# Output projection of a hybrid layer: both halves at the end in seven Strassen products, with weight sums made during group B

## The chip, the cores and the metric

One core of a Trainium2 chip runs the whole kernel. The metric is the device time of one launch in microseconds (us). The kernel before was run three times: median 1801.79 us, from 1801.08 to 1802.45. A further execution was profiled, and all rows below come from that one.

## The reference, cut to what matters

One layer over 1024 tokens of width 2048, in float32:

```python
xn = rms_norm(h, norm_w)
proj = xn @ w_in                                   # (1024, 2048) @ (2048, 7184)
...                                                # o_a: gated delta rule over 8 heads, gated by z_A
...                                                # o_b: chunked spatial gating over 8 groups, gated by z_B
mix = jnp.concatenate([o_a, o_b], axis=-1) @ w_out # (1024, 2048) @ (2048, 2048)
h = h + mix
return rms_norm(h, final_norm_w)
```

`o_a` (1024 columns) comes from group A, `o_b` (1024 columns) from group B. The change concerns the product with `w_out`, the residual sum and the final norm.

## The kernel before, in words

**Tiling.** Tokens are worked in two halves of 512 (`hf` 0 and 1, `T` = 512), each of four tiles of 128 tokens (`NT` = 4). The contraction of 2048 is cut into 16 steps of 128 (`KT` = 16). Every large product is made in three matmuls per step: each operand is split into a high part (a copy rounded to fp32r, on ACT, line 134) and a low part (source minus high part, on DVE, line 135), and TensorE (PE) adds high by high, high by low and low by high. `split` (lines 132 to 135) does this for 128x512 tiles.

**Stages.** `program` (line 910) runs, for each half, group A (the q, k, v and z columns, pair by pair of heads), group B (24 chunks of `v_b`, then 16 projections for u and z) and `out_phase(hf)`. So the order is A(0), B(0), out(0), A(1), B(1), out(1). Each stage is a generator of chunks: a prep that loads a 256 KB piece of weights and splits it, and an mm that issues its matmuls. `run` (line 211) keeps three preps ahead of the matmuls. A projection is four chunks of 12 matmuls of 128x512 (`project`, line 247).

**Tasks.** All other work (gates, convolutions, the solve and the recurrence of the delta rule, the spatial gating, evacuation of results) is written as generators that `spawn` queues and `tick` (called once or more in each chunk) advances; `yield n` lets n ticks pass. The recurrence of a pair of heads (`task_pair`, line 545) is a chain between PE and DVE: `p` (line 617, PE) reads the state, `vz` (line 620, DVE) follows, `ds` (line 628, PE) uses it, and `state` (line 629, DVE) is updated for the next `p`. The recurrence of the last pair of a half runs while group B's first chunks are multiplied.

**What sets the order.** A build-time scheduler fixes one order of instructions per engine, and each engine works its list in order. SP issues the loads of weights (`w_chunk`, line 182: three raw buffers `wr`, four of `wh` and of `wl`), the loads of x and the stores of `mix`. POOL issues the loads of `fw` and the `swapo` copies. An instruction that waits on SP or DVE holds up all that stands behind it on that engine.

**Buffers.** A tag names a ring of buffers that several users share; the next user of a buffer waits until the last one is done with it. The tags that the change speaks of are `cv` (3 buffers of 256 KB), `bv` (2), `z` (2), `pc` (4), the activation tiles `ah` and `al` (16 each) and `b8` (4 of 1 MB). PSUM has 3 banks for projections, 2 `p1`, 1 `ds` and 2 general ones.

**Output phase.** `out_phase(hf)` (line 839) takes four column blocks (`cb`) by 16 steps `k`; each chunk loads 256 KB of `w_out` (`wro`), splits it (`who`, `wlo`) and issues for each of the four token tiles three matmuls (lines 891 to 893, result `oa`): 768 matmuls of 128x512 per half. In block 0 each step also loads the half's `mix` tile (`mr`, on ACT's queue) and splits it (`mh`, `ml`), once for the half. `task_out` (line 800) evacuates a block: for each token tile it loads the residual (`xres`, SP, tag `z`), adds the PSUM result (DVE, line 806), squares it with a row sum (ACT, line 808), and multiplies by the norm's weight `fw` (POOL, line 810). After the last block come the row scale and the stores (lines 812 to 837). In the second half the last block's last token tile is multiplied at the very end by itself, so that only one tile's finish follows the last matmul.

The functions that the change touches, with the line numbers of the profile:

Of the kernel before, what the change touches and what calls it, by code (L numbers as in the profile page):

```python
# [8 lines left out]
F32 = mybir.dt.float32  # L9
F32R = mybir.dt.float32r  # L10
# [21 lines left out]
def kernel(ctx, tc, x_tok, x_t, w_in, w_v0, w_vb, w_out, conv_w, norm_w, a_log, dt_bias,  # L32
# [84 lines left out]

    mix_d = [dr.tile([2 * H, P, T], F32, name=f"mix_d{i}", bufs=1) for i in range(NHALF)]
# [141 lines left out]
    def first_tiles(hf, xs, env, done):  # L260
# [3 lines left out]
        for q in range(KT // 2):  # L264
# [22 lines left out]
            def mm(ws, q=q):  # L287
                hi, lo, (vh, vl) = ws
                if q == 0:
                    accs.extend(proj_bank(f"first{hf}_{i}") for i in range(3))  # L290
                    accs.extend(ps.tile([P, T], F32, tag="p1", bufs=2, name=f"first{hf}_{i}") for i in (3, 4))
                    accs.append(ps.tile([P, T], F32, tag="ds", bufs=1, name=f"first{hf}_5"))
# [161 lines left out]
    W_EM = 5  # L454

# [308 lines left out]
    def group_b(hf, xs, st):  # L764

        env, sb = {}, {}
        for blk in range(1, 4):
# [32 lines left out]
    def task_out(hf, cb, acc, env, ts):  # L800
        for t in ts:
            h, ss, st = env["h"][t], env["ss"][:, t, :], env["st"][:, t, :]
            xr = wk.tile([P, T], F32, tag="z", bufs=2, name=f"xres{hf}_{cb}_{t}")
            nc.sync.dma_start(xr, x_tok[hf * NT + t, :, cb * T:(cb + 1) * T])
            hs = h[:, cb * T:(cb + 1) * T]
            nc.vector.tensor_tensor(hs, xr, acc[t], op=ALU.add)
            sq = wk.tile([P, T], F32, tag="o", bufs=2, name=f"sqh{hf}_{cb}_{t}")
            nc.scalar.activation(sq, hs, AF.Square, accum_out=ss[:, cb:cb + 1])
            if cb < 3:
                nc.gpsimd.tensor_tensor(hs, hs, env["fw"][cb], op=ALU.mult)  # L810
            if cb == 2:
                nc.vector.tensor_reduce(st[:, 0:1], ss[:, 0:3], axis=AX.X, op=ALU.add)
                nc.vector.tensor_scalar(st[:, 0:1], st[:, 0:1], DM * EPS, None, op0=ALU.add)
            if cb == 3:
                yield 1

                a, m, y, w = (st[:, i:i + 1] for i in range(1, 5))
                nc.vector.tensor_scalar(a, ss[:, 3:4], st[:, 0:1], 1.0 / DM, op0=ALU.add, op1=ALU.mult)
                nc.vector.tensor_scalar(m, ss[:, 3:4], st[:, 0:1], -0.5 / DM, op0=ALU.add, op1=ALU.mult)
                nc.vector.tensor_scalar(y.bitcast(I32), a.bitcast(I32), -0.5, 1597463007.0, op0=ALU.mult, op1=ALU.add)  # L820
                for _ in range(3):
                    nc.vector.scalar_tensor_tensor(w, y, m, y, op0=ALU.mult, op1=ALU.mult)
                    nc.vector.scalar_tensor_tensor(y, w, 1.5, y, op0=ALU.add, op1=ALU.mult)
                r0 = hf * T + t * P
                for q in (0, 2, 1, 3):
                    cs = slice(q * T, (q + 1) * T)
                    if q < 2:
                        nc.scalar.activation(h[:, cs], h[:, cs], AF.Copy, scale=y)
                    elif q == 2:
                        nc.vector.tensor_scalar(h[:, cs], h[:, cs], y, None, op0=ALU.mult)  # L830
                    else:
                        nc.vector.scalar_tensor_tensor(h[:, cs], h[:, cs], y, env["fw"][q], op0=ALU.mult, op1=ALU.mult)
                    if len(ts) == 1:
                        nc.sync.dma_start(out[r0:r0 + P, cs], h[:, cs])
                    elif q % 2:
                        c2 = slice((q - 1) * T, (q + 1) * T)
                        nc.sync.dma_start(out[r0:r0 + P, c2], h[:, c2])

    def out_phase(hf):


        env = {"mx": [], "w": {}}
        end = hf == NHALF - 1
        spare = [("kd", 3), ("gae", 3), ("ut", 2), ("pc", 4), ("cv", 3), ("wq", 2), ("bv", 2), ("rb", 1)]
        spare = [tb for tb in spare for _ in range(tb[1])]

        def keep(k):

            if k >= KT - 4 or k < 2:
                return None  # L850
            return [wk.tile([P, 1, T], F32R, tag=tag, bufs=bufs, name=f"wk{i}_{k}")
                    for i, (tag, bufs) in enumerate(spare[2 * k - 4:2 * k - 2])]

        def prep(cb, k, late):
            if late:
                return env["w"][k]
            w = w_chunk(w_out[cb, k], [P, 1, T], f"o{hf}_{cb}_{k}", keep(k) if end and cb == 3 else None)
            env["w"][k] = w
            if cb == 0:
                mr = wk.tile([P, T], F32, tag="cv", bufs=3, name=f"mr{hf}_{k}")  # L860
                nc.scalar.dma_start(mr, mix_d[hf][k])
                mh = act.tile([P, T], F32R, tag="ah", name=f"mh{hf}_{k}")
                ml = act.tile([P, T], F32R, tag="al", name=f"ml{hf}_{k}")
                split(mh, ml, mr)
                env["mx"].append((mh, ml))
            return w

        def mm(w, cb, k, late, k1):
            hi, lo = w
            if cb == 0 and k == 0:  # L870
                env["h"] = [big.tile([P, DM], F32, tag="b8", name=f"h{hf}_{t}") for t in range(NT)]
                env["ss"] = sm.tile([P, NT, 4], F32, tag="ssh", bufs=1, name=f"ssh{hf}")
                env["st"] = sm.tile([P, NT, 5], F32, tag="sth", bufs=1, name=f"sth{hf}")
                env["fw"] = []
                for c in range(4):
                    f = wk.tile([P, T], F32, tag=("bv", "bv", "kc", "kc")[c], bufs=2, name=f"fw{hf}_{c}")
                    nc.gpsimd.dma_start(f, fn_w[c * T:(c + 1) * T].partition_broadcast(P))
                    env["fw"].append(f)
            if k == 0:
                if cb % 2 == 0:  # L880
                    acc = [proj_bank(f"oa{hf}_{cb}_{t}") for t in range(3)]
                else:
                    acc = [ps.tile([P, T], F32, tag="p1", bufs=2, name=f"oa{hf}_{cb}_{t}") for t in range(2)]
                    acc += [ps.tile([P, T], F32, tag="ds", bufs=1, name=f"oa{hf}_{cb}_2")]
                env["acc"] = acc + [gen_bank(f"oa{hf}_{cb}_3")]
            acc = env["acc"]
            mh, ml = env["mx"][k]
            ts = (NT - 1,) if late else range(NT - 1) if end and cb == 3 and k > 1 else range(NT)
            for t in ts:
# [4 lines left out]
                if t == 1:  # L894
                    tick()
            if k == k1:
                spawn(task_out(hf, cb, acc, env, ts))
            tick()

        def chunk(cb, k, late=False, k1=KT - 1):  # L900
            return (lambda: prep(cb, k, late)), (lambda w: mm(w, cb, k, late, k1))
# [60 lines left out]
```

## Time and profile before

| what | value |
|---|---|
| runs, median (lowest to highest) | 1801.79 us (1801.08 to 1802.45) |
| the profiled execution, its own time | 1797.83 us |
| its span, first to last instruction | 1796.1 us |
| PE busy | 1763.2 us, 98% of the span |
| DVE / ACT / POOL busy | 1152.3 / 731.9 / 265.1 us |
| mean granted clock | 0.997 of full speed |

Busy time is the sum over an engine's instructions; two that overlap in its pipeline count once. The span is shorter than the execution's own time by what lies around the first and last instruction. In the rows, L12 is line 12 of the kernel, `out<-in` are the program's names, and brackets give idle time before an instruction and what ended it. Numbers in buffer names are mostly left out.

### The profile page before, as it was taken

What the parts mean: (1) busy time and instruction counts of PE and PEld (TensorE: products, weight loads), DVE (VectorE), ACT (ScalarE), POOL (GpSimd) and SP (SyncE); (2) the same over time, 40 slices, a digit from 0 to 9 for tenths busy, and PEclk for the clock granted to TensorE, in tenths of its full rate; (3) what the DMA queues carried; (4) which work ended last, traced back from release to release, by engine and by line L of the source; (5) the groups of instructions that cost most, each with busy time, mean ns of one, the idle gap of its engine ahead of it and who ended that gap; (6) DMA issues with size and microseconds to landing.
All of it is one profiled execution on the core that took longest, in us unless ns stands there. A gap on an engine that the chain in (4) does not pass through costs nothing.

```text
span 1796.1 us, 27364 instructions
## 1 busy us (share of the span) xinstructions
PE 1763.2 (98%) x9526; PEld 1488.7 (83%) x9526; DVE 1152.3 (64%) x2797; ACT 731.9 (41%) x1658; POOL 265.1 (15%) x318
## 2 busy tenths in 40 slices
PE   9999999999999999999999899999999999999997
PEld 8778788887998888888898788878889988888886
DVE  7798787988646334433757988979886554344344
ACT  7543544444343223423646445344443432233232
POOL 3210121211201100011302101212012020001110
PEclk9999999999999999999999999999999999999999
DMA  7455344364424434644455453543534243355443
GB/s 235 129 133 143 106 135 135 94 178 115 136 84 120 124 105 136 222 118 126 131 198 141 121 141 103 147 120 106 162 112 135 76 117 116 102 153 169 124 140 138
DMA packets 166458, 239.16 MB, mean 133 GB/s; under 512 B 35472, under 2 KB 68272, under 8 KB 166064
## 3 DMA queue, kind: packets, MB, share of 16 engines
q1 hardware_dynamic: 156704, 215.35, 41.1%
q0 software_dynamic: 4864, 13.67, 3.1%
q10 hardware_dynamic: 4752, 8.40, 1.5%
q8 instruction: 74, 1.21, 0.3%
q14 instruction: 64, 0.52, 0.1%
HBM read 200.61 MB, written 36.73 MB: 132 GB/s over the span
## 4 chain that ended last, share of the span: by engine, by line
PE 79%; DVE 12%; DMA 4%; ACT 2%; issue 2%; SPq 0%; POOL 0%; DVEq 0%; ACTq 0%; POOLq 0%
PE acc L236 14%; PE acc L239 14%; PE acc L237 14%; PE vb L783 8%; PE oa L891 6%; PE oa L893 6%; PE oa L892 6%; DVE wl L135 2%; DVE cv L410 2%; PE ds L628 1%; DMA wr<-w_in 1%; PE p L617 1%; DVE fs L564 1%; DVE fst L562 1%; PE sp L740 1%
## 5 line engine op out<-in xcount | busy, mean ns | idle before, releaser
L236 PE MATMUL acc<-xh,wh 128*128 128x512 f32 x1472 | 591.3, 402 | 1.3 <-ACT wh L134 1.3
L239 PE MATMUL acc<-xh,wl 128*128 128x512 f32 x1472 | 576.4, 392 | 7.0 <-DVE wl L135 6.8
L237 PE MATMUL acc<-xl,wh 128*128 128x512 f32 x1472 | 575.3, 391 | 0.0
L134 ACT CAST wh<-wr 128x512 fp32r<-128x512 f32 x368 | 225.8, 618 | 432.4 <-PE acc L237 319.8
L135 DVE TENSOR_TENSOR wl<-wr,wh 128x512 fp32r<-128x512 f32 x368 | 255.8, 697 | 156.8 <-ACT wh L134 155.4
L239 PEld LDWEIGHTS acc<-xh,wl 128*128 128x128 f32 x1472 | 276.8, 188 | 66.4 <-DVE wl L135 8.5
L236 PEld LDWEIGHTS acc<-xh,wh 128*128 128x128 f32 x1472 | 277.4, 188 | 57.3 <-issue 3.7
L237 PEld LDWEIGHTS acc<-xl,wh 128*128 128x128 f32 x1472 | 277.4, 188 | 51.9 <-issue 0.7
L891 PE MATMUL oa<-who,mh 128*128 128x512 f32 x472 | 183.6, 389 | 0.0
L892 PE MATMUL oa<-wlo,mh 128*128 128x512 f32 x472 | 183.6, 389 | 0.0
L893 PE MATMUL oa<-who,ml 128*128 128x512 f32 x472 | 183.6, 389 | 0.0
L135 DVE TENSOR_TENSOR wlo<-wro,who 128x512 fp32r<-128x512 f32 x118 | 88.4, 751 | 141.5 <-ACT who L134 141.4
L134 ACT CAST who<-wro 128x512 fp32r<-128x512 f32 x118 | 73.0, 620 | 143.8 <-PE oa L893 135.3
L410 DVE SCALAR_TENSOR_TENSOR cv<-pc,cw,cv 128x511 f32<-128x511 f32 (+1 forms) x144 | 108.5, 754 | 8.5 <-ACT cv L407 6.9
L783 PE MATMUL vb<-whvb,xh 128*128 128x256 f32 x384 | 110.5, 288 | 0.0
L783 PE MATMUL vb<-whvb,xl 128*128 128x256 f32 x384 | 108.6, 283 | 0.0
L783 PE MATMUL vb<-wlvb,xh 128*128 128x256 f32 x384 | 108.6, 283 | 0.0
L892 PEld LDWEIGHTS oa<-wlo,mh 128*128 128x128 f32 x472 | 88.6, 188 | 18.6
L893 PEld LDWEIGHTS oa<-who,ml 128*128 128x128 f32 x472 | 88.6, 188 | 18.4
L891 PEld LDWEIGHTS oa<-who,mh 128*128 128x128 f32 x472 | 88.6, 188 | 18.2
L564 DVE TENSOR_TENSOR fs<-fs,fst 32x31 f32<-32x31 f32 (+15 forms) x248 | 89.2, 360 | 4.1
L562 DVE TENSOR_TENSOR fst<-fs 32x31 f32<-32x31 f32 (+15 forms) x248 | 88.9, 359 | 4.2
(239 smaller groups left out, 2369.6 us busy)
## 6 DMA issues: line engine op xcount, KB each, us to landing
wr<-w_in SPq DMA_DIRECT2D x368, 256.0 KB, 3.1
wro<-w_out SPq DMA_DIRECT2D x128, 256.0 KB, 2.7
wrvb<-w_vb SPq DMA_DIRECT2D x48, 256.0 KB, 2.7
xr<-x_t SPq DMA_DIRECT2D x32, 256.0 KB, 3.7
mr<-mix_d ACTq DMA_DIRECT2D x32, 256.0 KB, 3.2
xres<-x_tok SPq DMA_DIRECT2D x32, 256.0 KB, 3.5
out<-h SPq DMA_DIRECT2D x14, 512.0 KB, 3.5
v0r<-w_v SPq DMA_DIRECT2D x16, 272.0 KB, 4.7
```

What stands on the lines that cost most here:

```text
L134: nc.scalar.copy(hi, src)
L135: nc.vector.tensor_tensor(lo, src, hi.bitcast(F32), op=ALU.subtract)
L236: nc.tensor.matmul(acc, hi[:, kk, :], xh, start=(k == 0), stop=False)
L237: nc.tensor.matmul(acc, hi[:, kk, :], xl, start=False, stop=(last and lo is None))
L239: nc.tensor.matmul(acc, lo[:, kk, :], xh, start=False, stop=last)
L410: nc.vector.scalar_tensor_tensor(cv[:, s:], acc[:, :T - s], w, cv[:, s:], op0=ALU.mult, op1=ALU.add)
L562: nc.vector.tensor_tensor(tv, bc(lu[:, k, k + 1:].unsqueeze(2), [32, n, m]), bc(xu[:, k:k + 1, 0:m], [32, n, m]), op=ALU.mult)
L564: nc.vector.tensor_tensor(xu[:, k + 1:, 0:m], xu[:, k + 1:, 0:m], tv, op=ALU.subtract)
L783: nc.tensor.matmul(a, l[:, tsl], r[:, k % 2, :], start=fl, stop=sp_, skip_group_check=True)
L891: nc.tensor.matmul(acc[t], mh[:, tsl], hi[:, 0, :], start=(k == 0), stop=False)
L892: nc.tensor.matmul(acc[t], mh[:, tsl], lo[:, 0, :], start=False, stop=False)
L893: nc.tensor.matmul(acc[t], ml[:, tsl], hi[:, 0, :], start=False, stop=(k == k1))
```

## The change

`out_phase(0)`, which stood between the halves, is gone, and one `out_phase()` at the end multiplies both halves. The product of 1024x2048 by 2048x2048 is cut into four quarters of `mix` (token half by contraction half), four of `w_out` (contraction half by column half) and four of the result `c`, and Strassen's seven products of quarters are made in place of eight. Each product has two column blocks, eight steps, four token tiles and three matmuls. Five products need a sum of two quarters of `mix` (made on DVE before the split) and five a sum of two quarters of `w_out`. A product's result is added to or subtracted from one or two quarters of `c` (line 908 of the changed kernel); the first to reach a quarter takes the residual `xres` in place of `c`. The quarters of `c` live in the `al` and `b8` tiles, the split tiles of `mix` in the tags of groups A and B, and `fw` in `pc`.

The sums of `w_out`'s quarters are made by a new task, `w_sums`, spawned at the start of each group B, 40 units in each. A unit is two loads of 256 KB on SP (`wsa` in tag `cv`, `wsb` in `bv`), one add on DVE (line 842 of the changed kernel) and one store on POOL's queue to a DRAM buffer `wc_d` (line 843), from which the end phase loads it as it loads `w_out` otherwise. The first loads come 30 ticks into group B, a unit every three ticks from there. Two of the first six banks of `first_tiles` are taken in another order.

```diff
+    wc_d = dr.tile([5, 2, KT // 2, P, T], F32, name="wc_d", bufs=1)
...
+    W_SUM0 = 30
...
     def group_b(hf, xs, st):
         env, sb = {}, {}
+        units = [(n, cb, k) for n in SUMS for cb in range(2) for k in range(HK)]
+        spawn(w_sums(units[hf * len(units) // 2:(hf + 1) * len(units) // 2]))
...
+    PRODUCTS = (
+        (((0, 0),), ((0, 1), (1, 1), -1), ((0, 1, 1), (1, 1, 1))),
+        (((0, 1), (0, 0), 1), ((1, 1),), ((0, 0, -1), (0, 1, 1))),
+        (((0, 1), (1, 1), -1), ((1, 0), (1, 1), 1), ((0, 0, 1),)),
+        (((0, 0), (1, 1), 1), ((0, 0), (1, 1), 1), ((0, 0, 1), (1, 1, 1))),
+        (((1, 1),), ((1, 0), (0, 0), -1), ((0, 0, 1), (1, 0, 1))),
+        (((1, 0), (1, 1), 1), ((0, 0),), ((1, 0, 1), (1, 1, -1))),
+        (((1, 0), (0, 0), -1), ((0, 0), (0, 1), 1), ((1, 1, 1),)),
+    )
...
+    def w_sums(units):
+        def load(u):
+            n, cb, k = u
+            a, b, _ = PRODUCTS[n][1]
+            ta = wk.tile([P, 1, T], F32, tag="cv", bufs=3, name=f"wsa{n}_{cb}_{k}")
+            tb = wk.tile([P, 1, T], F32, tag="bv", bufs=2, name=f"wsb{n}_{cb}_{k}")
+            nc.sync.dma_start(ta, w_quarter(a, cb, k))
+            nc.sync.dma_start(tb, w_quarter(b, cb, k))
+            return ta, tb
+        yield W_SUM0
+        nxt = load(units[0])
+        for i, (n, cb, k) in enumerate(units):
+            (ta, tb), nxt = nxt, (load(units[i + 1]) if i + 1 < len(units) else None)
+            yield 3
+            nc.vector.tensor_tensor(ta, ta, tb, op=op[PRODUCTS[n][1][2]])
+            nc.gpsimd.dma_start(wc_d[SUMS.index(n), cb, k], ta.rearrange("p o c -> p (o c)"))
...
+        def evac(n, cb, accs, ts):
+            for t in ts:
+                for ci, cl, sign in PRODUCTS[n][2]:
...
+                    src = c
+                    if new:
+                        src = wk.tile([P, T], F32, tag="z", bufs=2, name=f"xres{n}_{cb}_{t}_{ci}{cl}")
+                        nc.sync.dma_start(src, x_tok[ci * NT + t, :, (cl * 2 + cb) * T:(cl * 2 + cb + 1) * T])
+                    nc.vector.tensor_tensor(c, src, accs[t], op=op[sign])
+                    if final[ci, cl] == n:
+                        yield from finish(n, ci, cl, cb, t, c, len(ts) < NT)
+                if t != ts[-1]:
+                    yield 1
...
             yield from group_b(hf, xs, st)
-            yield from out_phase(hf)
+        yield from out_phase()
```

A row of `PRODUCTS` gives the quarters of `mix`, those of `w_out` (with the sign of the second) and the quarters of `c` that the product goes to, with their signs. `finish` (not shown) does what lines 808 to 837 did, quarter by quarter.

**SP's order in group B of half 0.** Before, from the last chunk of `v_b` to the first of the projections (`wr0_32_1` is the second chunk of the first projection of group B, `wr0_40_0` the first chunk of the second one):

```order
L185 DMA wrvb0_3_7_5710<-w_vb 128x512
L185 DMA wr0_32_0_5759<-w_in 128x512
L185 DMA wr0_32_1_5805<-w_in 128x512
L185 DMA wr0_32_2_5851<-w_in 128x512
L185 DMA wr0_32_3_5937<-w_in 128x512
L185 DMA wr0_40_0_5972<-w_in 128x512
```

Now, from the same place, with what each load waits for (DMASW is the landing of a transfer of POOL's queue, here the store of an earlier unit; DVE, PE and DMAHW are semaphores of those engines and of the other DMA queues):

```order
L186 DMA wr0_32_1_5850<-w_in 128x512 [waits DMAHW1_49,DVE_49]
L835 DMA wsb0_0_0_5402<-w_out 128x512 [waits PE_49]
L186 DMA wr0_32_2_5902<-w_in 128x512 [waits DMAHW6_49,DMAHW2_49,DVE_49]
L835 DMA wsb0_0_1_5406<-w_out 128x512 [waits DMAHW7_49,DMAHW5_49,DVE_49]
L835 DMA wsb0_0_2_5464<-w_out 128x512 [waits DMAHW0_49,PE_49]
L834 DMA wsa0_0_3_5511<-w_out 128x512 [waits DMASW1_49]
L835 DMA wsb0_0_3_5512<-w_out 128x512 [waits DMAHW7_49,DVE_49]
L835 DMA wsb0_0_4_5576<-w_out 128x512 [waits DMAHW3_49,DMAHW0_49,DVE_49]
L186 DMA wr0_32_3_5994<-w_in 128x512 [waits DMAHW4_49,DVE_49]
L834 DMA wsa0_0_4_5575<-w_out 128x512 [waits DMASW2_49]
L835 DMA wsb0_0_5_5648<-w_out 128x512 [waits DMAHW6_49,DMAHW2_49,DVE_49]
L834 DMA wsa0_0_5_5647<-w_out 128x512 [waits DMASW3_49]
```

Eight loads for the sums now stand between chunks 2 and 4 of the weights, and from the fourth unit on each `wsa` waits for a store on POOL's queue.

**DVE's order in the recurrence of the last pair of half 0.** Before (`state`, `vz`: the chain described above; `va`, `rv`, `rst` are the layer norm's scalars of group B):

```order
L629 SCALAR_TENSOR_TENSOR state<-state,gam_921,ds_3_1_2_5929 128x128
L721 TENSOR_TENSOR va_5899<-mv_5897,rstd 128x4
L620 TENSOR_TENSOR vz_1_119<-ut_3_0_5701,p_0_3_0_3_5932 64x128
L722 TENSOR_TENSOR va_5899<-va_5899,rstd 128x4
L135 TENSOR_TENSOR wl_32_3_5940<-wr_32_3_5937,wh_32_3_5939 128x512
L723 TENSOR_SCALAR va_5899<-va_5899 128x4
L629 SCALAR_TENSOR_TENSOR state<-state,gam_921,ds_3_0_3_5950 128x128
```

Now:

```order
L632 SCALAR_TENSOR_TENSOR state<-state,gam_922,ds_3_1_2_5980 128x128
L724 TENSOR_TENSOR va_5950<-mv_5948,rstd 128x4
L623 TENSOR_TENSOR vz_1_119<-ut_3_0_5740,p_0_3_0_3_5983 64x128
L725 TENSOR_TENSOR va_5950<-va_5950,rstd 128x4
L842 TENSOR_TENSOR wsa_0_7_5800<-wsa_0_7_5800,wsb_0_7_5801 128x512
L726 TENSOR_SCALAR va_5950<-va_5950 128x4
L136 TENSOR_TENSOR wl_32_3_5997<-wr_32_3_5994,wh_32_3_5996 128x512
L126 TENSOR_SCALAR rv_5949<-va_5950 128x4
L127 TENSOR_SCALAR rsm_v_5959<-va_5950 128x4
L632 SCALAR_TENSOR_TENSOR state<-state,gam_922,ds_3_0_3_6007 128x128
```

The add of unit 7 (`wsa_0_7`, the eighth) now stands ahead of a low part of weights and of the state update from which the next `p` reads.

## Rows read from the trace of the kernel before

**Rows 1.** The page: busy time, share of the span and instructions of each engine.

```profile
PE 1763.2 (98%) x9526; PEld 1488.7 (83%) x9526; DVE 1152.3 (64%) x2797; ACT 731.9 (41%) x1658; POOL 265.1 (15%) x318
```

**Rows 2.** Waits of PE: engine, line, waited for, us in total, times, longest.

```profile
PE acc L239 <- DVE wl L135: 6.8, 2, 5.0
PE ds L628 <- DVE vz L620: 4.8, 13, 0.9
```

**Rows 3.** Windows of the span: busy time of each engine, granted clock, DMA share, GB/s.

```profile
core 0: us, PE busy (x) PEld busy (x) DVE busy (x) ACT busy (x) POOL busy (x), PEclk, DMA share, GB/s
0.00:45.00 45.00, 43.78 (x260) 39.87 (x261) 34.36 (x55) 31.51 (x61) 17.71 (x31) 1.00 0.74 235
500.00:620.00 120.00, 119.00 (x738) 103.56 (x738) 61.38 (x152) 40.99 (x96) 17.11 (x19) 1.00 0.38 111
721.00:895.00 174.00, 174.00 (x769) 144.11 (x768) 79.44 (x121) 71.60 (x131) 28.65 (x25) 1.00 0.48 147
...
1612.00:1787.00 175.00, 174.74 (x771) 144.35 (x770) 72.67 (x130) 56.91 (x107) 18.77 (x13) 1.00 0.46 141
```

**Rows 4.** Timeline of PE, end of the first output phase: start, us, instruction.

```profile
879.67 0.39 PE L891 MATMUL oa<-who,mh 128*128 128x512 f32 x1
...
895.08 0.39 PE L893 MATMUL oa<-who,ml 128*128 128x512 f32 x1
```

**Rows 5.** DMA issues in group B of half 0, 500 to 620 us: count, KB, us to landing.

```profile
wr<-w_in SPq DMA_DIRECT2D x34, 256.0 KB, 3.0
...
fw<-fn_w POOLq DMA_DIRECT2D x2, 256.0 KB, 3.7
```

**Rows 6.** DMA in a crowded stretch, 721 to 741 us: GB/s of its slices, packets, issues.

```profile
GB/s 209 283 217 266 291 311 283 287 320 348 332 156 152 303 414 410 410 377 373 397 410 393 393 397 459 340 348 287 307 86 57 266 225 74 266 205 74 311 406 291
DMA packets 3155, 5.87 MB, mean 293 GB/s; under 512 B 365, under 2 KB 365, under 8 KB 3153
...
wro<-w_out SPq DMA_DIRECT2D x5, 256.0 KB, 4.8
xres<-x_tok SPq DMA_DIRECT2D x2, 256.0 KB, 6.4
...
fw<-fn_w POOLq DMA_DIRECT2D x1, 256.0 KB, 5.5
```

**Rows 7.** Timelines of POOL and SP in group B of half 0: issues of DMAs.

```profile
560.50 2.99 POOL L427 DMA_DIRECT2D swapo<-ut  x4 [1.05 <-DVE ut L422]
...
573.70 0.33 SPq L144 DMA_DIRECT2D xr<-x_t  x1
```

**Rows 8.** Timeline of PE in group B of half 0.

```profile
513.26 1.06 PE L602 MATMUL up<-bv,tt 128*128 128x128 f32 x8
...
534.98 0.41 PE L617 MATMUL p<-state,wq 128*128 128x128 f32 x2
...
640.54 0.39 PE L236 MATMUL acc<-xh,wh 128*128 128x512 f32 x1
```

**Rows 9.** Groups of DVE and ACT by form, 721 to 895 us: busy, mean ns, idle before.

```profile
L135 DVE TENSOR_TENSOR wlo<-wro,who 128x512 fp32r<-128x512 f32 x61 | 45.9, 755 | 69.4 <-ACT who L134 69.4
...
L806 DVE TENSOR_TENSOR h<-xres,oa 128x512 f32<-128x512 f32 x13 | 8.6, 683 | 2.5 <-DMA xres<-x_tok 2.5
L135 DVE TENSOR_TENSOR ml<-mr,mh 128x512 fp32r<-128x512 f32 x10 | 6.9, 690 | 9.8 <-ACT mh L134 9.8
...
L134 ACT CAST who<-wro 128x512 fp32r<-128x512 f32 x61 | 37.6, 618 | 69.8 <-PE oa L893 66.5 <-DMA wro<-w_out 2.6 <-PE acc L237 0.7
```

**Rows 10.** The page: DMA issues of the whole span, us to landing.

```profile
xres<-x_tok SPq DMA_DIRECT2D x32, 256.0 KB, 3.5
```

**Rows 11.** Timeline of the end of the program.

```profile
1786.36 0.39 PE L893 MATMUL oa<-wk,ml 128*128 128x512 f32 x1
...
1790.69 1.79 SPq L834 DMA_DIRECT2D out<-h  x4
```

**Rows 12.** Timeline of PE in group A of half 1.

```profile
993.64 0.79 PE L239 MATMUL acc<-xh,wl 128*128 128x512 f32 x1 [5.04 <-DVE wl L135]
```

More of the change, by code (lines that the diff above doesn't have):

```diff
@@ L289, in mm @@
                 if q == 0:
-                    accs.extend(proj_bank(f"first{hf}_{i}") for i in range(3))
-                    accs.extend(ps.tile([P, T], F32, tag="p1", bufs=2, name=f"first{hf}_{i}") for i in (3, 4))
-                    accs.append(ps.tile([P, T], F32, tag="ds", bufs=1, name=f"first{hf}_5"))
+                    accs.extend(proj_bank(f"first{hf}_{i}") for i in range(2))
+                    accs.extend(ps.tile([P, T], F32, tag="p1", bufs=2, name=f"first{hf}_{i}") for i in (2, 3))
+                    accs.append(ps.tile([P, T], F32, tag="ds", bufs=1, name=f"first{hf}_4"))
+                    accs.append(proj_bank(f"first{hf}_5"))
                 for k2 in range(2):
@@ L797, in group_b @@
             yield from project(hf, 5 * H + g, xs, lambda acc, g=g: spawn(task_zb(hf, g, env["vn"], sb, acc)))
[L800 to L858, printed above, removed]
-            if cb == 0:
[L860 to L874, printed above, removed]
@@ L886, in mm @@
             acc = env["acc"]
-            mh, ml = env["mx"][k]
-            ts = (NT - 1,) if late else range(NT - 1) if end and cb == 3 and k > 1 else range(NT)
-            for t in ts:
+            ah, al = env["a"][k]
+            for i, t in enumerate(ts):
                 tsl = slice(t * P, (t + 1) * P)
-                nc.tensor.matmul(acc[t], mh[:, tsl], hi[:, 0, :], start=(k == 0), stop=False)
-                nc.tensor.matmul(acc[t], mh[:, tsl], lo[:, 0, :], start=False, stop=False)
-                nc.tensor.matmul(acc[t], ml[:, tsl], hi[:, 0, :], start=False, stop=(k == k1))
-                if t == 1:
+                nc.tensor.matmul(acc[t], ah[:, tsl], hi[:, 0, :], start=(k == 0), stop=False)
+                nc.tensor.matmul(acc[t], ah[:, tsl], lo[:, 0, :], start=False, stop=False)
+                nc.tensor.matmul(acc[t], al[:, tsl], hi[:, 0, :], start=False, stop=(k == HK - 1))
+                if i == 1:
@@ L895, in mm @@
                     tick()
[L896 to L901, printed above, removed]
-        for cb in range(4):
-            for k in range(KT):
-                yield chunk(cb, k)
-        if end:
-            for k in reversed(range(2, KT)):
-                yield chunk(3, k, True, 2)
+            if k == HK - 1:
+                spawn(evac(n, cb, acc, ts))
@@ new lines, in mm, with first_mm @@
+            if len(ts) != 1 or k % 2:
+                tick()
+        kept = {}
+        def first_mm(w, k):
+            kept[k] = w
+            mm(w, LAST, 1, k, range(2))
+        for n in range(LAST + 1):
+            for cb in range(2):
+                for k in range(HK):
+                    if n == LAST and cb == 1:
+                        yield (lambda k=k: prep(LAST, 1, k)), (lambda w, k=k: first_mm(w, k))
+                    else:
+                        yield (lambda n=n, cb=cb, k=k: prep(n, cb, k)), \
+                            (lambda w, n=n, cb=cb, k=k: mm(w, n, cb, k, range(NT)))
@@ L910, in program @@
+        for t in range(2, NT):
+            for k in range(HK):
+                yield (lambda: None), (lambda w, k=k, t=t: mm(kept[k], LAST, 1, k, (t,)))
     def program():
```

107 lines of the change are left out of this document (100 added, 7 removed).

## The prediction

> **What bounds the kernel now.** I read the page's busy times first, then the waits of PE, the windows by stage, the timelines around the change, and the landings of transfers. The reader is to see that TensorE (PE) is busy 1763.2 of 1796.1 us [rows 1] and waits little (its two largest waits are 6.8 and 4.8 us [rows 2]). In the output phase it never waits: 174.00 of 174 us at a granted clock of 1.00, with DVE at 79 and the DMA engines at 0.48 [rows 3]. So fewer matmuls there are time saved, as long as everything that feeds them stays ahead. Group B is nearly as dense (119.00 of 120 us), with transfers at only 111 GB/s [rows 3].
>
> The runs' median of 1801.79 lies 3.96 above the profiled execution's 1797.83; I sum against the latter and add 3.96 at the end. A measurement of this kernel can tell about 0.2% (3.6 us) from no change.
>
> **The matmuls removed.** Two phases of 768 matmuls (4 blocks x 16 steps x 4 tiles x 3) become 7 products x 2 blocks x 8 steps x 4 tiles x 3 = 1344, of the same shape: 192 fewer. From 879.67 to 895.08 lie 68 of them, 15.41 us, 0.2266 us each [rows 4]. 192 x 0.2266 = **-43.5 us**.
>
> **The weight sums in group B.** This term decides the result. Each half adds 80 loads (SP), 40 adds (DVE) and 40 stores (POOL's queue) of 256 KB. PE's work stays as it is; the question is whether the units run through in time. A `wsa` buffer is one of three: it is loaded, added into and stored, and the load of the third unit after it waits for that store, on SP, where loads of `w_in` stand behind it. So add number i+3 comes one ring time T after add i. T is load + add + store + hand-overs.
>
> - Load: 3.0 us in this stretch, 4.8 where the transfers run at 293 GB/s [rows 5, 6].
> - Add: 0.68, as the residual's add of the same size [rows 9].
> - Store: no row shows a 256 KB store on POOL's queue. The nearest are the `fw` loads on that queue, 3.7 here and 5.5 in the crowded stretch [rows 5, 6]. Issuing adds 0.75 (2.99 for four copies [rows 7]).
> - Hand-overs between engines: three; no row shows them alone, I choose 0.3 together.
>
> That is T = 8.4 from the quiet rows and 12.0 from the crowded ones. Taking the issue to lie within the landing it is 7.7 and 11.3; I keep 7.7 and 12 as the ends. The quiet end contradicts itself: three units per 7.7 us are nine transfers of 262 KB, 306 GB/s, and with the 111 of group B 417 GB/s, where the best slices of the crowded stretch hold about 410 and its mean is 293 [rows 6]. At T = 10 they make 236 + 111 = 347 GB/s, between that mean and those best slices. The crowded stretch is one of bursts from three queues, while here at most three units are on their way, so I take **T = 10**.
>
> The Trainium skill ("DMA: Bandwidth & Descriptors", section "Anatomy of one DMA — SWDGE (gpsimd) path") fits one transfer of that path as about 2.0 us plus its bytes at 436 GB/s. That would be 2.6 us for each 256 KB, an estimated T of 6.2 to 6.9, and almost no stall: the sum would be near -40 and not what I get below. The rows disagree with that fit here: `fw` took 3.7 us where the stretch was quiet [rows 5].
>
> What a late unit costs. The first `wsb` waits for the `bv` buffer that the last pair's `up` reads at 513.3 [rows 8], which with a load puts add 0 at about 518.3 and add 1, behind the next `bv`, at 522.7. Two places count, each with its order shown above.
>
> - *Early:* add 7 is 522.7 + 2T. On DVE it stands ahead of the state update from which the `p` of 534.98 reads [rows 8]; PE, in order, waits there. It is late by 2T - 12.3.
> - *Late:* add 39 is 518.3 + 13T. On SP its `wsa` stands ahead of the fourth weight chunk of the projection whose matmuls start at 640.54 [rows 8]. That load must go out by about 635.2 (640.54 less a landing of 4.0 between 3.0 and 4.8, less 0.62 for the cast and 0.7 for the low part [rows 9]); the add follows its own load by 5.5, so it is late by 518.3 + 13T - 640.7 = 13T - 122.4.
>
> The larger of the two is the stall of a half, since a stall at the first place gives the second as much more time. T = 7.7: 3. T = 10: 8 (13T gives 7.6, 2T 7.7). T = 11: 21. T = 12: 34. Both halves: **+16 us** (6 to 67). Up to T = 9.4 the late place costs nothing; past it each us of T costs 26.
>
> **The output phase itself.** A product is 192 matmuls, 43.5 us of PE. DVE has in it 16 low parts of weights at 0.755, on average 8 low parts of `mix` at 0.69, 5 to 6 sums of `mix` quarters at 0.68 (40 in all) and 14 evacuations (96 in all) at 0.683 [rows 9]: 12.1 + 5.5 + 3.9 + 9.4 = 31 us, 71%. Before it was 79.44 of 174, 46%; the start of the program holds DVE at 39.87 of 45 with PE at 43.78 [rows 3], so 71% can be borne, though a block of 21.8 us that has both splits and double evacuations takes about 22. Products 0 and 1 load 24 residuals through two `z` buffers; a token tile with two targets uses both, so three of the four loads of a block come in series: 3 x 3.5 [rows 10] + 8 x 0.683 + about 1 = 17 of 21.8 us. ACT has about as many casts as before (112 + 56 for 128 + 32) and POOL as many products with `fw`. I take **+2** (0 to 10, the upper end a shortage of about 1 us per product and some).
>
> **Edits with small prices.** A(1) now follows B(0) directly: `first_tiles` must get its weights and x behind B(0)'s loads instead of behind the output phase's, and the sums end about there: **+1** (0 to 6, two landings of 3.0). The end of the program: before, 4.3 us from the start of the last matmul to the last stores' issue [rows 11]; the chain afterwards is again one tile's square, scalars, scalings and stores, with one more add per tile: **+0.5** (-1 to 3). The 5.0 us for which PE waits in A(1) [rows 2, 12] may move either way, since that half's tasks now start from other conditions; taken at nothing (-5 to +3).
>
> **Sum.** -43.5 + 16 + 2 + 1 + 0.5 = -24. 1797.8 - 24 = 1773.8 for a profiled execution, +3.96 = 1777.8 for the median: **1778 us**.
>
> **The rivals.**
>
> - *The sums' ring sets the pace (slower).* SP is the place: a `wsa` waits for a store on POOL's queue, and the weights of the projections queue behind it. If T is 12, as the crowded rows add up with the issue counted, both halves lose 2 x 33.6 = 67 us: 1801.8 - 43.5 + 67 + 3.5 = 1829. It makes the kernel slower from T = 10.9 (2 x (13T - 122.4) > 40). For it: at T = 10 the traffic would already be above the mean at which 4.8 and 5.5 us were measured. Against: that stretch had transfers of three queues in bursts, and a ring of three slows itself. Chance 0.15.
> - *The output phase waits for residuals.* If the loads of `xres` take 6.4 us as in the crowded row [rows 6], three in series and the adds make 3 x 6.4 + 5.5 + 1 = 25.7, 4 over a block of 21.8, at some three block ends: 12 more, 1790. For it: the phase's loads come on SP's one list, behind weights that wait for buffers. Against: the median over the program is 3.5 [rows 10]. Chance 0.12.
> - *Every cover holds.* With T = 7.7 or less the halves lose 6 us or nothing: 1801.8 - 43.5 + 3 + 3.5 = 1765. By the fit of the Trainium skill the ring is never late, and this is the case it would give. For it: group B has 0.6 of the DMA engines' time free [rows 3], and only traffic of the change's own would crowd it. Against: 417 GB/s. Chance 0.13.
>
> That the matmuls are not fewer is no rival: the count of 1344 is fixed by the program.
>
> **How the numbers follow.** The forecast, T from about 8.5 to 10.5 and small prices as taken, has 0.60; it gives 1766 to 1795. The range takes it with the residual rival and most of the full cover: 1760 to 1803, which leaves out the ring rival and little else, under 2 in 10. Faster by over 0.2%: the forecast, the residuals and the cover less a margin, 0.79. Within 0.2%: 0.06, with T between 10.8 and 11.1. Slower: 0.15.
>
> **What would show it.** Right: 1344 matmuls of `oa` in a dense stretch of about 304 us at the end (1344 x 0.2266), PE idle of about 8 us in each group B, after the `p` of its last recurrence (ended by DVE, behind an add of line 842) or before late projections (ended by weights whose load came late), SP waiting for stores, and landings of `wsa`, `wsb` near 4 and of the stores near 5 us. Wrong: idle PE of 20 us or more in either group B with stores of 5.5 or more (the ring), gaps in the last stretch ended by `xres` or DVE (the residuals), or a PE that waits nowhere (the cover). A longer stretch per matmul than 0.2266 in the output phase would break the first term itself.

## The result, and the profile after

The changed kernel took 1825.25 us (median of 4 runs, 1823.58 to 1829.67) against 1801.43 for the kernel before in the same comparison: a ratio of 1.014, 95% interval 1.0117 to 1.0162. It is slower by 1.4%, where 1778 and a gain were forecast. The profiled execution has a span of 1823.4 us, 27.3 more than before's 1796.1.

Busy times of the changed kernel, from the page (as [rows 1]):

```profile
PE 1739.9 (95%) x9334; PEld 1460.5 (80%) x9334; DVE 1267.0 (69%) x2985; ACT 733.3 (40%) x1670; POOL 307.0 (17%) x394
```

PE has 192 matmuls fewer and 23.3 us less work, and yet the span grew. Where PE stood, from its waits in the changed kernel (as [rows 2]; L numbers are now those of the changed kernel, 1 to 5 above the old ones in groups A and B):

```profile
PE acc L240 <- DVE wl L136: 27.4, 16, 3.8
PE at L648 <- DVE s L745: 17.0, 2, 8.7
PE ds L631 <- DVE vz L623: 10.7, 17, 2.5
PE p L620 <- DVE va L724: 4.0, 2, 2.2
```

Each of these is ended by DVE. Windows cut at the stages of the changed kernel (columns as in [rows 3]): group B of half 0, group B of half 1, the output phase.

```profile
453.07:754.49 301.42, 276.07 (x1588) 239.28 (x1587) 160.75 (x340) 90.44 (x190) 54.97 (x76) 0.97 0.68 212
1205.13:1504.42 299.29, 274.28 (x1587) 236.82 (x1586) 155.27 (x329) 82.60 (x174) 53.31 (x75) 0.98 0.67 209
1504.42:1813.80 309.38, 306.01 (x1345) 251.87 (x1343) 212.20 (x384) 125.17 (x241) 34.76 (x25) 1.00 0.56 173
```

The same two windows of the kernel before:

```profile
453.18:721.23 268.05, 267.06 (x1587) 234.62 (x1586) 129.94 (x292) 84.08 (x176) 31.14 (x35) 1.00 0.41 119
1344.67:1612.66 267.99, 267.20 (x1588) 234.79 (x1587) 131.38 (x288) 84.22 (x176) 30.30 (x35) 1.00 0.40 114
```

So group B grew by 33.4 and 31.3 us. PE stands idle 25 us in each (301.42 - 276.07, 299.29 - 274.28) where it was 1 before, and the same 1587 or 1588 matmuls are busy 9.0 and 7.1 us longer: for 17.1 and 10.2 us of the two stretches the granted clock is the lower of its two levels (1.2 in place of 2.4 GHz), which gives the averages of 0.97 and 0.98 where it was 1.00. The output phases fell from 2 x 174.1 to 309.4, by 38.8. Group A of half 1 grew by 1.2, the end by 0.3. Together: 33.4 + 31.3 - 38.8 + 1.2 + 0.3 = 27.4, within rounding the whole difference of 27.3.

One undisturbed turn of a `wsa` buffer, from the timelines of DVE, POOL, SP and DVE: the add of the fourth unit, its store's issue, the load of the seventh unit into the same buffer, its add.

```profile
527.36 0.69 DVE L842 TENSOR_TENSOR wsa<-wsa,wsb 128x512 f32<-128x512 f32 x1 [3.56 <-DMA wsb<-w_out]
528.35 0.54 POOL L843 DMA_DIRECT2D wc_d<-wsa  x1 [4.77 <-DVE state L632]
532.93 0.33 SPq L834 DMA_DIRECT2D wsa<-w_out  x1
537.49 0.69 DVE L842 TENSOR_TENSOR wsa<-wsa,wsb 128x512 f32<-128x512 f32 x1 [2.43 <-DMA wsa<-w_out]
```

From the add to its store's issue 0.99, to the next load's issue 4.58, to the next add 4.56: together 10.1 us, the T = 10 of the forecast. But the 40 adds of half 0 run from 516.9 to 666.9, 13 turns of 11.5 on average; half of these turns take over 11.1 us, the longest 17.4. One of the longer ones, from DVE's timeline, with the first thing that PE does behind it:

```profile
580.30 0.69 DVE L842 TENSOR_TENSOR wsa<-wsa,wsb 128x512 f32<-128x512 f32 x1 [1.45 <-DMA wsb<-w_out]
...
588.80 0.75 DVE L671 SCALAR_TENSOR_TENSOR o<-ut,hnw,z 128x512 f32<-128x512 f32 x1 [5.44 <-DMA ut<-swapo]
589.47 0.69 DVE L842 TENSOR_TENSOR wsa<-wsa,wsb 128x512 f32<-128x512 f32 x1
590.07 0.75 DVE L745 SCALAR_TENSOR_TENSOR s<-sp,lnw,brow 128x512 f32<-128x512 f32 x1
```

```profile
590.96 0.55 PE L648 MATMUL at<-ut,gae 128*128 128x128 f32 x1 [8.69 <-DVE s L745]
```

DVE waits 5.4 us for a head's output to come back from its transposing copy. That copy went out late (at 574.84, before the change at 560.50), since the DVE steps ahead of it (the head's norm) stood behind adds that waited for their loads, up to 2.4 us each. It was also longer on its way: 13.9 us from the issue out to the landing back, where it was 9.8 before. Behind the wait stand an add and `s`, which frees the bank that PE's `at` needs. Here the wait for one transfer of the recurrence and the waits for the sums' transfers have locked into one chain. Of the 50 us for which PE stands in the two groups B, 22 end behind such a wait for a head's copy (8.7 and 3.5 in half 0, 8.3 and 1.7 in half 1).

Most of the rest stands in the second half of group B, where PE waits for low parts of weights. One of these waits (2.3 us, ended at 646.22), from DVE's timeline:

```profile
644.87 0.69 DVE L842 TENSOR_TENSOR wsa<-wsa,wsb 128x512 f32<-128x512 f32 x1 [2.53 <-DMA wsa<-w_out]
645.48 0.69 DVE L136 TENSOR_TENSOR wl<-wr,wh 128x512 fp32r<-128x512 f32 x1
```

The weight had landed at 642.20 and its high part was done at 642.92. The low part stood behind an add that waited for its load.

Landings, from the page (as [rows 5, 6]):

```profile
wr<-w_in SPq DMA_DIRECT2D x368, 256.0 KB, 3.5
wsa<-w_out SPq DMA_DIRECT2D x80, 256.0 KB, 4.2
wsb<-w_out SPq DMA_DIRECT2D x80, 256.0 KB, 4.2
wc_d<-wsa POOLq DMA_DIRECT2D x80, 256.0 KB, 4.6
```

Loads of 4.2 and stores of 4.6 lie between the quiet and the crowded rows, as taken. So what had to be found was why the loss was 65 us and not 16, with the sums' transfers as fast as assumed.

### The profile page after: what moved, and what is told of

It is laid out like the page before. It is cut to its first block, busy times and chain, and to the rows that moved or that the text cites. A ratio compares the mean times of both kernels' runs of the same rounds, so it can differ in the third digit from the quotient of the medians.

```text
span 1823.4 us, 27717 instructions
## 1 busy us (share of the span) xinstructions
PE 1739.9 (95%) x9334; PEld 1460.5 (80%) x9334; DVE 1267.0 (69%) x2985; ACT 733.3 (40%) x1670; POOL 307.0 (17%) x394
## 5 line engine op out<-in xcount | busy, mean ns | idle before, releaser
L240 PE MATMUL acc<-xh,wl 128*128 128x512 f32 x1472 | 582.0, 395 | 27.4 <-DVE wl L136 27.4
L971 PE MATMUL oa<-wlo,a 128*128 128x512 f32 x432 | 168.6, 390 | 3.3 <-DVE wlo L136 3.3
L972 PE MATMUL oa<-who,a 128*128 128x512 f32 x432 | 168.2, 389 | 0.0
L970 PE MATMUL oa<-who,a 128*128 128x512 f32 x432 | 168.2, 389 | 0.0
L842 DVE TENSOR_TENSOR wsa<-wsa,wsb 128x512 f32<-128x512 f32 x80 | 58.2, 728 | 97.9 <-DMA wsb<-w_out 53.8
L136 DVE TENSOR_TENSOR wlo<-wro,who 128x512 fp32r<-128x512 f32 x108 | 80.6, 750 | 43.8 <-ACT who L135 43.7
L135 ACT CAST who<-wro 128x512 fp32r<-128x512 f32 x108 | 66.5, 617 | 82.0 <-PE oa L972 44.1
L971 PEld LDWEIGHTS oa<-wlo,a 128*128 128x128 f32 x432 | 81.1, 188 | 21.9 <-DVE wlo L136 5.0
L972 PEld LDWEIGHTS oa<-who,a 128*128 128x128 f32 x432 | 81.1, 188 | 16.7
L970 PEld LDWEIGHTS oa<-who,a 128*128 128x128 f32 x432 | 81.1, 188 | 16.7
```

Source lines behind the costliest of these rows:

```text
L135: nc.scalar.copy(hi, src)
L136: nc.vector.tensor_tensor(lo, src, hi.bitcast(F32), op=ALU.subtract)
L240: nc.tensor.matmul(acc, lo[:, kk, :], xh, start=False, stop=last)
L842: nc.vector.tensor_tensor(ta, ta, tb, op=op[PRODUCTS[n][1][2]])
L970: nc.tensor.matmul(acc[t], ah[:, tsl], hi[:, 0, :], start=(k == 0), stop=False)
L971: nc.tensor.matmul(acc[t], ah[:, tsl], lo[:, 0, :], start=False, stop=False)
```

## The experiments

Three theories stood at the start. RING: three `wsa` buffers passing through load, add and store set the pace. TRAFFIC: the added bytes lengthen the landings of the weights themselves. BLOCKED DVE: adds that wait for their loads hold what stands behind them on DVE. After the first four runs a fourth took their place, CONVOY. A median of before in one comparison is that of its own chip (1797.6 to 1801.4); where a run has one time only, stages of the trace are compared.

### No sums

```diff
-        spawn(w_sums(units[hf * len(units) // 2:(hf + 1) * len(units) // 2]))
...
-            src = w_quarter(PRODUCTS[n][1][0], cb, k) if n not in SUMS else \
-                wc_d[SUMS.index(n), cb, k].rearrange("p (o c) -> p o c", o=1)
+            src = w_quarter(PRODUCTS[n][1][0], cb, k)
```

Expected: 

> Leaves out the sums of w_out's quarters altogether (no loads, adds or stores in group B); the end phase loads the first quarter of each pair in place of the sum, so five of the seven products are other numbers of the same size. This prices the sums as a whole. In the changed kernel the stretch from the first v_b matmul to the next stage is 301.4 and 299.3 us, before it was 268.0 in both halves. Every theory that puts the loss into the sums expects both stretches back at 268 to 269 and a time of 1825.3 - 33.4 - 31.3 = about 1761. If the loss were in the end phase or in group A, it would stay above 1790.

Measured: 1761.15 us (one run; before 1799.69 on that chip). Windows of this run, both groups B and the output phase:

```profile
452.51:720.90 268.39, 267.06 (x1587) 234.65 (x1586) 134.64 (x300) 91.14 (x190) 32.31 (x36) 1.00 0.42 121
1171.60:1439.73 268.13, 267.08 (x1587) 234.63 (x1586) 130.87 (x289) 82.98 (x174) 30.24 (x35) 1.00 0.40 116
1439.73:1749.80 310.07, 307.25 (x1345) 252.87 (x1343) 213.10 (x385) 125.65 (x241) 35.06 (x25) 0.99 0.56 173
```

Group B is as before, the output phase as in the change. The whole loss in group B belongs to the sums.

### No store

```diff
-            nc.gpsimd.dma_start(wc_d[SUMS.index(n), cb, k], ta.rearrange("p o c -> p (o c)"))
...
```

Expected: 

> Leaves out the 80 stores of the sums (loads and adds stay; the end phase loads the first quarter of each pair, as in the run without sums). Theory RING (pace set by three cv buffers through load, add, store; T measured 10.0 to 10.5 where undisturbed): without the store T is load 4.3 + add 0.7 + hand-over, about 6, so 13T - 122.4 and 2T - 12.3 are both below zero and nothing is left of the stall, about 1763 to 1770. Theory TRAFFIC (all landings are longer because the DMA engines are full): a third of the added bytes goes, the stall shrinks by about a third, 1800. Theory BLOCKED DVE (adds wait for their loads in DVE's fixed order and hold what stands behind): loads are as late as before behind the two bv buffers, at least half of the early stalls stay (some 8 us per half), 1777 or more.

Measured: 1786.05 us (one run). From the first `v_b` matmul to the next stage it takes 279.4 and 281.6 us, so of 33.4 and 31.3 us 11 and 14 are left. Waits of PE and of DVE:

```profile
PE at L648 <- DVE s L745: 11.1, 2, 5.7
```

```profile
DVE wsa L842 <- DMA wsb<-w_out: 61.3, 45, 3.3
```

RING alone would have left nothing. What is left fits BLOCKED DVE: DVE still waits 61.3 us for the sums' loads, and PE for DVE. But 40 of the 65 us went with the store (and with a third of the sums' bytes), so the store is a part of the loss that BLOCKED DVE alone does not explain.

### Adds on POOL

```diff
-            nc.vector.tensor_tensor(ta, ta, tb, op=op[PRODUCTS[n][1][2]])
+            nc.gpsimd.tensor_tensor(ta, ta, tb, op=op[PRODUCTS[n][1][2]])
```

Expected: 

> The 80 adds go from DVE to POOL, all else as in the change. BLOCKED DVE: nothing of DVE waits for loads of the sums any more; the stalls ended by DVE (2.5, 2.2 and 8.7 us in half 0, 1.4, 1.2, 1.8 and 8.3 in half 1) go, 1825 - 26 = 1799 or a little less with the clock's share. RING: POOL's add of this size takes about 1.6 in place of 0.7 us, T grows by 0.9 to about 11.3 and the late stall grows by 13 x 0.9 = 12 us per half, so the whole is 1825 or more. Both can hold at once: then about 1820, with the early stalls gone and the late ones longer.

Measured: 1851.61 us (one run), group B 315.9 and 309.8 us. Waits of PE:

```profile
PE acc L240 <- DVE wl L136: 19.5, 4, 7.8
PE acc L237 <- ACT wh L135: 18.7, 11, 5.2
PE at L648 <- DVE s L745: 17.5, 2, 9.2
```

and of SP:

```profile
SPq L834 <- DMA wc_d<-wsa: 91.0, 52, 4.3
SPq L835 <- POOL wsa L842: 82.0, 55, 3.6
```

The expectation that DVE's stalls would go failed: `at` waits as long as before. The adds now hold POOL's list, and with it the head's output and its copies; and 18.7 us are ended by the weights' cast, that is by weights whose loads went out late on SP, behind its waits for stores and for the adds on POOL. Moving the wait to another in-order list moved the stall and made it longer (an add takes 1.36 us there).

### Loads tied to the projections' chunks

The program asks for a unit every three ticks, which is one and a half chunks, but the build need not keep that distance: in SP's new order above eight loads of the sums stand between chunks 2 and 4 of the weights. So a true dependence was put in: DVE copies one column of the present chunk's low part into the `wsb` buffer, and the load has to follow. The start goes from tick 30 to tick 51.

```diff
     def mm_chunk(acc, w, xs, q):
+        paced["lo"] = w[1]
...
+            nc.vector.tensor_copy(tb[:, 0, 0:1], paced["lo"][:, 0, 0:1].bitcast(F32))
             nc.sync.dma_start(tb, w_quarter(b, cb, k))
```

Expected: 

> All sums are made as in the change, but each unit's second load is tied to the weights' chunk that is multiplied at that point of the program (DVE first copies one column of that chunk's low part into the wsb buffer; the load follows), from the fourth chunk of the projections on. So a unit comes every one and a half chunks, 4.07 us, over the whole of group B, where in the change the build placed one every 3.05 us from the recurrence on. RING as the limit together with a placement that is faster than the ring: a unit may now take T = 12.2, the ring of 10.4 keeps up, and both stretches come back to 268 to 272, 1762 to 1772. TRAFFIC: the bytes are the same over a longer stretch, 193 + 111 = 304 GB/s in place of 370, landings stay near 4.5 and half of the loss stays, 1790. If placement is not the point, 1825.

Measured: 1843.1 us (median of 4), ratio 1.0218, 1.0175 to 1.0262. None of the theories had this. Group B is 305.9 and 303.6 us although a unit now has 4.07 us in the program; in the trace one comes every 5.6. One turn late in half 0, SP's timeline first, then DVE's:

```profile
702.98 0.37 SPq L839 DMA_DIRECT2D wsb<-w_out  x1
...
708.63 0.33 SPq L186 DMA_DIRECT2D wr<-w_in  x1
711.56 0.33 SPq L837 DMA_DIRECT2D wsa<-w_out  x1
712.00 0.51 SPq L186 DMA_DIRECT2D wr<-w_in  x1
712.59 0.38 SPq L839 DMA_DIRECT2D wsb<-w_out  x1
```

```profile
707.31 0.69 DVE L846 TENSOR_TENSOR wsa<-wsa,wsb 128x512 f32<-128x512 f32 x1 [5.72 <-DMA wsb<-w_out]
707.92 0.68 DVE L136 TENSOR_TENSOR wl<-wr,wh 128x512 fp32r<-128x512 f32 x1
...
717.08 0.69 DVE L846 TENSOR_TENSOR wsa<-wsa,wsb 128x512 f32<-128x512 f32 x1 [5.35 <-DMA wsb<-w_out]
```

This is a loop: the add at 707.31 has waited 5.7 us for the load of 702.98; its store lands before 711.56, where SP goes on with the next `wsa`; `wr` and `wsb` stand behind that; the add at 717.08 (the second one on; another stands at 709.41) waits for this `wsb`, 9.8 us after the first. In each turn only three weight chunks pass, since their loads (SP) and low parts (DVE) stand between the waits, and PE needs 2.72 us for a chunk (12 matmuls of 0.2266), 8.2 for three. The weights move at the pace of the sums' round trip. Giving a unit more room did not help here, where the add stands right behind its loads. This is the theory CONVOY.

### Adds spaced as well

The add gets a second operand of 1.0 that is made from a later chunk (its low part times 0 plus 1), so that it cannot be placed before that chunk. Both loads of a unit are tied now, the start stays at tick 51, and the program asks for the next unit's loads one tick before an add, not three (the loop is not shown). The edit, against the tied run:

```diff
+            nc.vector.tensor_copy(ta[:, 0, 0:1], paced["lo"][:, 0, 0:1].bitcast(F32))
             nc.sync.dma_start(ta, w_quarter(a, cb, k))
...
-            nc.vector.tensor_tensor(ta, ta, tb, op=op[PRODUCTS[n][1][2]])
+            one = sm.tile([P, 1], F32, tag="w1", bufs=2, name=f"w1_{n}_{cb}_{k}")
+            nc.vector.tensor_scalar(one, paced["lo"][:, 0, 0:1].bitcast(F32), 0.0, 1.0, op0=ALU.mult, op1=ALU.add)
+            nc.vector.scalar_tensor_tensor(ta, ta, one, tb, op0=ALU.mult, op1=op[PRODUCTS[n][1][2]])
```

Expected: 

> All sums are made with the engines, queues and buffers of the change. Beside the loads (both now tied to the projections' chunk as in the tied run) the add too is tied to a chunk, two chunks after its loads, and the next load of the same buffer follows two and a half chunks after the add; a unit still comes every one and a half chunks. Theory CONVOY: the loss comes from in-order lists in which weights' loads (SP) and low parts (DVE) stand directly behind a wait for the sums' own transfers, at distances shorter than the transfers take (the build had put an add right behind its loads, which land 4.4 us later, and a load right behind a store, which lands 3.3 to 4.6 us later). Now the distances are 5.4 us for a load and 6.8 us for a store, and nothing waits for long: group B back to 268 to 273 us, 1763 to 1775. Theory TRAFFIC (the added bytes lengthen the weights' own landings): same bytes, the stall stays as in the tied run, 1830 or at least above 1800.

Measured: 1773.78 us (median of 4, 1772.99 to 1778.79), before 1798.21 on that chip: ratio 0.9862, 0.984 to 0.9883. Group B takes 274.5 and 273.3 us. The same stretch, 640 to 721 us, in this run and in the tied run:

```profile
640.00:721.00 81.00, 81.00 (x371) 67.47 (x370) 46.10 (x108) 21.15 (x35) 14.21 (x20) 1.00 0.89 293
```

```profile
640.00:721.00 81.00, 69.40 (x308) 54.85 (x307) 35.19 (x67) 16.90 (x28) 12.20 (x19) 1.00 0.75 240
```

With the DMA engines busier (0.89, 293 GB/s) PE does not wait at all in this run; in the tied one (0.75, 240) it is idle 11.6 us. The sums' landings are even longer here, 4.5, 4.8 and 4.5 us for `wsa`, `wsb` and `wc_d`, and the weights' own loads land in 4.6 us in both groups B, where the change had 4.4 and 4.0 and the kernel before 2.9 in half 0. So neither TRAFFIC nor RING by itself makes the bulk of the loss: the same three buffers, engines and queues carry the same 40 units in each half.

What the expectation had wrong is that "nothing waits for long". DVE's waits for the sums, in the change and in this run:

```profile
DVE wsa L842 <- DMA wsb<-w_out: 53.8, 27, 5.4
DVE wsa L842 <- DMA wsa<-w_out: 41.1, 22, 4.1
```

```profile
DVE wsa L846 <- DMA wsb<-w_out: 63.8, 45, 5.0
DVE wsa L837 <- DMA wc_d<-wsa: 24.2, 18, 3.3
```

That is 94.9 and 88.0 us, nearly the same, but PE stands 50 us in the groups B of the change and 10 here. The turns of a buffer are even longer, 14.8 and 14.3 us on average. So neither the sum of DVE's waits nor the length of a turn is the price. The reading left is that it counts what stands behind a wait and how soon PE needs it.

Group B keeps 6.4 and 5.3 us more than before. PE's one large stall there is at `at` (4.2 and 4.5 us), and the copy of the head ahead of it is 12.4 and 12.6 us on its way, against 9.8 in the run without sums. The added bytes may have this part; no run isolates it.

### More buffers

```diff
-            ta = wk.tile([P, 1, T], F32, tag="cv", bufs=3, name=f"wsa{n}_{cb}_{k}")
-            tb = wk.tile([P, 1, T], F32, tag="bv", bufs=2, name=f"wsb{n}_{cb}_{k}")
+            ta = wk.tile([P, 1, T], F32, tag=("cv", "kd")[late and i % 2], bufs=3, name=f"wsa{n}_{cb}_{k}")
+            tb = wk.tile([P, 1, T], F32, tag=("bv", "wq")[late and i % 2], bufs=2, name=f"wsb{n}_{cb}_{k}")
```

Expected: 

> As the run before, with six buffers for the first operand (cv and kd in turn) and four for the second (bv and wq) from the seventh unit on, and loads two units ahead from the ninth, so 9.5 us from load to add and some 15 us from store to the buffer's next load. CONVOY: as e5_spaced or a few us better, where e5's distances were still too short; 1762 to 1770. If the ring of three buffers as such were the limit (RING), only this one and not e5_spaced would come back. TRAFFIC: no change against e5_spaced, above 1800.

Measured: 1773.8 us (median of 4, 1770.59 to 1775.55), ratio 0.9861, 0.984 to 0.9883. From the ninth unit on the loads also go two units ahead (that loop is not shown). DVE's waits for the sums fall from 88.0 to 15.2 us, but group B takes 275.7 and 275.6: doubling the buffers and the distances gives nothing beyond the run before.

### Only the adds tied

The two copies into `ta` and `tb` of the spaced run are left out; the operand of 1.0 stays.

Expected: 

> As e5_spaced, but the loads are untied again: only the adds are tied to the projections' chunks, two chunks behind the place where the program asks for their loads. On SP the next load of a buffer again stands right behind the store it waits for; on DVE the add no longer stands right behind its loads. With the tied run (loads tied, adds not: 1843) this tells which in-order list carries the convoy. If DVE's wait for the loads carries it (low parts held behind the add): about as e5_spaced, 1772 to 1785, with SP waiting some 3 us per unit that the three raw weight buffers cover. If SP's wait for the stores carries it (weight loads held behind wsa): 1810 or more.

Measured: 1778.19 us (median of 4), ratio 0.9898, 0.9867 to 0.9928; group B 273.0 and 272.1 us. Waits of DVE and of SP in this run:

```profile
DVE wsa L844 <- DMA wsb<-w_out: 20.9, 22, 2.5
```

```profile
SPq L837 <- DMA wc_d<-wsa: 151.8, 67, 5.5
```

and in the tied run:

```profile
DVE wsa L846 <- DMA wsb<-w_out: 152.8, 59, 5.7
```

```profile
SPq L837 <- DMA wc_d<-wsa: 130.6, 58, 6.0
```

SP waits for the stores longer here than in the tied run, and PE is not held by it: it stands 4.5 and 3.5 us in the two groups B, nearly all at `at`. What differs is DVE: 20.9 us against 152.8. So in this order it is the place of the adds on DVE that carries the convoy, and tying them is enough to break it. That SP's wait is covered by the three raw weight buffers is a reading that no run tests. The run with adds on POOL shows that waits on SP can make weights late as well; what makes the difference was not isolated. The start at tick 51 is not the cure, since the tied run has it too; whether the place of the adds alone would have cured the units at their old pace was not tried.

### Transposing copies on ACT's queue

```diff
-            hd["ot"] = swap(y, o.rearrange("p t d -> p (t d)"), y, f"o{nm}", nc.gpsimd, True)
+            hd["ot"] = swap(y, o.rearrange("p t d -> p (t d)"), y, f"o{nm}", nc.scalar, True)
```

Expected: 

> As e5_spaced, but the copies that transpose a head's output (swapo out, ut back) are issued on ACT's queue instead of POOL's. In e5_spaced one stall of 4.2 and 4.5 us per half is left, where PE's at waits for a DVE list that waits for the copy back; POOL needs 3.0 us to issue the four copies out. If that chain's length is what is left, it gets 2 to 3 us shorter and each half gains 2 to 3 us with the clock, 1768 to 1771. If ACT's casts behind the issue become late instead, or the landings under load are what makes the chain long, no gain: 1774 or more.

Measured: 1810.0 us (median of 4), ratio 1.0067, 1.0049 to 1.0086. From ACT's timeline in group A:

```profile
248.58 1.26 ACTq L432 DMA_DIRECT2D swapo<-ut  x2
250.04 0.47 ACTq L435 DMA_DIRECT2D ut<-swapo  x1
250.55 1.26 ACTq L432 DMA_DIRECT2D swapo<-ut  x2
253.90 0.63 ACT L546 ACTIVATE z<-pcz 128x512 f32<-128x512 f32 x1 [13.19 <-DMA swapo<-ut]
254.44 0.60 ACT L135 CAST wh<-wr 128x512 fp32r<-128x512 f32 x1
```

The copy back waits for the copy out on ACT's list, and the weights' casts stand behind it; ACT had done no other work for 13.2 us. PE waits for these casts:

```profile
PE acc L237 <- ACT wh L135: 13.2, 5, 4.6
```

The same kind of wait now stands in a fourth engine's list, ahead of what PE needs. Group B of half 0 starts 13.5 us later than in the spaced run. That `at` still waits 3.0 and 3.2 us here says nothing clear on the stall that the run aimed at; how to remove the 4.2 and 4.5 us of the spaced run stays open.

## Why the prediction was wrong

- **Matmuls removed, -43.5; output phase, +2.** Nearly right. 2 x 174.1 became 309.4, -38.8 in place of -41.5. PE waits there 3.3 us for low parts of weights.
- **The weight sums, +16 (6 to 67).** This is the step that failed: they cost 64.7 us. The stage was right, and so were the single prices: 4.2 to load, 0.7 to add, 4.6 to store, and 10.1 us for an undisturbed turn. With T = 10.1 the forecast's own line gives 9 us for a half, not 33. What it had wrong is that the sums touch the critical work at two places only, each priced by how late one unit comes. They stand in the same in-order lists all along, and a wait of an add holds each time what stands behind it on DVE: low parts of weights, the recurrence and the steps of a head's output. The measured average of 11.5 would give 27 by that line, near the 33.4, but this proves nothing: in the spaced run the turns take 14.8 and 14.3 us and group B grows by 6.4 and 5.3.
- **The places.** The early one cost 5.4 us of PE in half 0 (0.8, 2.5 and 2.2 at `ds` and `p`) where 7.7 was worked out, but behind the adds of units 1, 3 and 6 and not behind that of unit 7. The late one was to come on SP, by a weight whose load goes out late. No wait of PE in group B was ended so: four waits of 7.2 us between 646 and 668 us were for low parts behind adds on DVE, and one of 3.5 at 627.53 stood behind a wait for a head's copy. The 8.7 us at `at` had not been named at all: no step looked at the transposing copy of the last heads, for whose way back DVE had already waited 2.3 us before the change.
- **The clock.** No term had it: 9.0 and 7.1 us of longer matmuls, a quarter of the 64.7. Before the change the granted clock stayed at 1.00 through group B.
- **Small terms.** Group A of half 1 +1.2 (taken +1), the end +0.3 (taken +0.5).
- **The rivals.** The ring rival, with 0.15, gave 1829 and the measurement is 1825. That it comes so near is luck: it put the stall on SP with T at 12 from crowded landings, but stores landed in 4.6 and not 5.5 us, PE waited for DVE, and the spaced run shows that this very ring can run without holding PE. The residual rival did not come: PE's output phase waits for low parts only. "Every cover holds" is what the spaced runs come near to.
- **The Trainium skill** ("DMA: Bandwidth & Descriptors", section "Anatomy of one DMA — SWDGE (gpsimd) path"): the store of 256 KB on POOL's queue landed in 4.6 us, 3.5 in the tied run, against the 2.6 that its fit gives, an estimate. The measurement decides. The forecast also put the loads of SP by this fit, which is for POOL's path; they landed in 4.2.

The chance of 0.79 for a gain rested on T as the only measure of the sums. With a break-even at 10.9 us and a price of 26 us for each us of T, even that term deserved a wider range upward, and the slower rival more than 0.15.

## What to carry to other kernels

A background stream of load, work and store that shares in-order lists with the critical stream is not priced by its bandwidth or its ring alone: ask, for each instruction that waits, how far it stands behind its transfer, and what of the critical stream stands behind it. Where a build decides the order, a pace written in ticks may not hold; a real dependence on the critical stream's own progress does. Here one small operand on each add (with a later start and later loads) turned 1.4% slower into 1.0% faster, and with the loads tied too into 1.4% faster, with the same bytes, buffers and engines.

## What the runs showed of the hardware

- Stalls of a few us cost more than their own length here. In the changed kernel PE's granted clock was 0.94 in the window below, in which the 8.7 us and a 3.5 us stall lie. PE had stood from 526.2 to 528.69 (the stall at `ds`) when the clock fell to its lower level, 1.2 GHz, at 529.38; until 532.8 the 128x256 matmuls of `vb` start every 0.21 us instead of every 0.12.

```profile
560.00:640.00 80.00, 67.81 (x313) 56.52 (x312) 45.04 (x86) 17.75 (x40) 26.14 (x36) 0.94 0.90 299
```

- Transfers at 293 GB/s and a share of 0.89 do not hold PE at all for 81 us of the spaced run, although DVE waits for them 28.1 us in that stretch.
- The add of two 128x512 tiles takes 0.69 us on DVE (median) and 1.36 on POOL (mean).
